# Scratch tiles placed by the plan, and the sums of the second norm's output made in the tiles of x

## The chip, the cores and the metric

The kernel runs on one core of a Trainium2 chip. The metric is the device time of one execution in microseconds (us), and lower is better. The kernel before takes 2038.9 us, the median of three runs (2038.4 to 2039.33). Engines go by their names in the profile: PE is TensorE, which multiplies matrices (PEld its weight loads), DVE is VectorE, ACT is ScalarE, POOL is GpSimd, and SP is SyncE, whose queue issues nearly all DMA transfers. Tiles lie in SBUF, with 128 partitions; matmuls write into PSUM, which has eight banks of 128 x 512 numbers.

## The reference, cut to what matters

The reference is a decoder trunk of two layers over 1024 tokens with 1024 channels, all in float32:

```python
for l in range(DEPTH):
    h = rmsnorm(x, attn_norm[l])
    proj = h @ w_in[l]                      # split into ten parts
    y_a = mla_attention(...)                # latent attention, 4 heads
    y_b = short_gated_conv(...)
    y_c = multiscale_pool(...)
    y_d = swa_sink_attention(...)           # sliding window
    mixed = ...                             # each group normed, times mix_norm
    x = x + mixed @ w_o[l]
    h2 = rmsnorm(x, ffn_norm[l])            # the second norm
    gate, up = jnp.split(h2 @ w_gate_up[l], 2, axis=-1)
    x = x + (jax.nn.silu(gate) * up) @ w_down[l]
return rmsnorm(x, final_norm)
```

where `rmsnorm(x, g)` is `x * rsqrt(mean(x * x) + eps) * g`. The change touches the second norm's output `h2`, in the form in which the gate and up products take it.

## The kernel before, in words

**Layout.** Activations are held transposed: channels on the 128 partitions, tokens along a row. A tile is 128 channels by 512 tokens, so x is eight channel blocks (d from 0 to 7) in two token halves (t is 0 or 1). Each float32 operand of a matmul is split into a high part, rounded to the matmul's input type by ACT, and the rest, which DVE gets by a subtraction (`split`, `half_split`, lines 362 to 380); `mm3` (line 344) then makes three matmuls of the parts.

**Stages of a layer.** First the combined projection and the four mixers, written interleaved; then the output projection with the residual (`out_part`, `out_last`), which leaves the new x in tiles `x[d][t]`, stores it to DRAM as `xr` (line 1271), squares it for the second norm, and splits it with the norm's gain into `hb`. Then the gate/up stage, in rounds over 22 blocks of the hidden channels, and then the down projection, which loads x again from `xr`.

**The gate/up products** go by a seven-product scheme for 2 x 2 blocks (channel parity by token half), in place of eight. Beside blocks of x it needs four combined blocks, called N1, N2, T3 and T4. `combine(j)`, line 1223, makes them for the channel blocks 2j and 2j + 1, so there are four rounds of it a layer. Of the round's four tiles of x, (a0, b0) is the even channel block in both token halves and (a1, b1) the odd one. With gains g0 and g1 it makes v0 = g0 b0 and v1 = g1 b1 on ACT (lines 1229 and 1230), and on DVE n1 = g0 a0 - v0 (line 1232), n2 = -n1 - v1 (line 1219, in `minus`), t3 = v1 - v0 (line 1238) and t4 = -g1 a1 - n2 (line 1240). Each of the four sums is then split (lines 364 and 367). At its end the four tiles of x are given back.

Between the rounds of `combine` the program has the first blocks' products: `plain` (line 1502) makes one block without the scheme, whose gates are multiplied by the norm (line 445), put through silu on ACT (line 1540), multiplied on POOL (line 1542) and multiplied with the up part on DVE (line 445 again); two further blocks, `early`, go through the scheme step by step (`start`, `n2`, `n1`, `t3`, `b22`, `t4`). `n2` needs N2 of all four rounds. The third such block, `GateUp(3)`, has its weights loaded at lines 1289 and 1291.

**Scratch.** Short-lived tiles of 128 x 512 numbers come from `tmp` (line 188), under one of three tags: `te`, with two buffers, `tn` and `tp`, with three each. A tile that asks for a buffer of its tag waits until the readers of that buffer's former tile are done. The longer-lived tiles come from 47 slots of two halves each (`Slots`, line 57; `u` in the profile); a slot is used again as the plan's times say.

**The order of the work** is the output of a planner that runs when the program is built (`Order`, `scheduled_kernel`, line 2210). The kernel is traced once with simple rules for places. A list scheduler with a cost for each instruction gives every instruction a planned end. From these ends come the PSUM bank of each `ps` tile (`banks`, line 2178) and the slots' uses; the kernel is traced again with them, scheduled again, and the order is improved with 30 tries of random changes (a fixed seed). This is done for two factors on the costs of DVE and ACT (`SLOW`, line 41); the version whose order takes least in six trials with random delays is kept, and its order is imposed on each engine's queue. The queues are worked off in that order on the chip: an instruction that waits holds up all behind it on its engine.

Of the kernel before, what the change touches and what calls it, by code (L numbers as in the profile page):

```python
# [14 lines left out]
F32 = mybir.dt.float32  # L15
F32R = mybir.dt.float32r
AF = mybir.ActivationFunctionType
ALU = mybir.AluOpType
AX = mybir.AxisListType

P = 128
# [3 lines left out]
HT = 512  # L25
# [9 lines left out]
B11, B21, B22, N1, N2, T3, T4, B12 = range(8)  # L35

HALVES = (1, 0)
OUT_PARTS = tuple((d, t) for d in range(NK) for t in HALVES)
N_U = 47
SLOW = (1.0, 1.03)  # L40
PREP = (1, 27)

# [83 lines left out]
def trunk_kernel(ctx: ExitStack, tc: tile.TileContext, ins, out, given=None, ends=None):  # L126
    nc = tc.nc
    act, dve, pe, pool, sp = nc.scalar, nc.vector, nc.tensor, nc.gpsimd, nc.sync
# [3 lines left out]
    tpool = ctx.enter_context(tc.tile_pool(name="tmp", bufs=6))  # L132
# [3 lines left out]

    slots = Slots(ctx.enter_context(tc.tile_pool(name="slots", bufs=1)), N_U, ends)
    R, F = View(slots, F32R), View(slots, F32)

    def rd(ap):  # L140
        return ap.bitcast(F32)
# [32 lines left out]
        "dc": deque(["t", "t", "mm", "mm"]),  # L174
    }

    bank_of = iter(given or ())

    def ps(tag):
        if tag in turns:  # L180
# [5 lines left out]
        return psum.tile([P, HT], F32, name=f"ps_{tag}", tag=b, bufs=1)  # L186

    def tmp(tag="te"):
        return tpool.tile([P, HT], F32, name=tag, tag=tag, bufs={"te": 2, "tn": 3, "tp": 3}[tag])

    def small(n):
        return spool.tile([P, n], F32, name=f"sm{n}", tag=f"sm{n}", bufs=16 if n < 16 else 2)
# [169 lines left out]
    def split(hi, lo, f, gain=None, after=None):  # L362
        if gain is None:
            a = act.copy(hi, f)  # L364
            if after is not None:
                behind(a, after)
            dve.tensor_tensor(out=lo, in0=f, in1=rd(hi), op=ALU.subtract)  # L367
        else:
            a = act.activation(hi, f, AF.Copy, scale=gain)  # L369
            dve.scalar_tensor_tensor(  # L370
                out=lo, in0=f, scalar=gain, in1=rd(hi), op0=ALU.mult, op1=ALU.subtract
            )
        return a

    def half_split(f, gain=None):
        h, l = R.half(), R.half()
        split(R.ap(h), R.ap(l), f, gain)
        return h, l
# [68 lines left out]
    def pcol(l, c, rows=slice(0, P)):  # L447
        return par[rows, l * PC_N + c : l * PC_N + c + 1]
# [65 lines left out]
    for l in range(L):  # L514
# [57 lines left out]
        if l == 0:  # L572
# [41 lines left out]
            for i in range(L):  # L614
                for o, c, n in ((nsink, PC_SINK, 4), (nffn, PC_FFN, NK)):
                    dve.tensor_scalar(
                        out=o[:, i * n : i * n + n],
                        in0=par[:, i * PC_N + c : i * PC_N + c + n],
                        scalar1=-1.0,
                        scalar2=None,  # L620
                        op0=ALU.mult,
# [17 lines left out]
        for t in range(2):  # L639
            f = tmp()  # L640
# [8 lines left out]
        for t in range(2):  # L649
            f = tmp()  # L650
# [5 lines left out]
            for g in range(2):  # L656
# [3 lines left out]
                    out=o[:, :, 1, :], in0=pv[:, :, g, :], in1=rd(o[:, :, 0, :]), op=ALU.subtract  # L660
# [187 lines left out]
        for ct in range(2):  # L848
            pp = nextp
            u, a, b = F.pair(), F.pair(), F.pair()  # L850
# [16 lines left out]
            else:  # L867
# [7 lines left out]
                out=dst,  # L875
                in0=src,
                scalar=cst[:, CC_INVW + ct : CC_INVW + ct + 1],
                in1=uf,
                op0=ALU.mult,
                op1=ALU.subtract,  # L880
# [28 lines left out]
        for m in range(2):  # L909
            pp = project() if m else nextp  # L910
            for t in range(2):
                f = tmp()
# [19 lines left out]
        for t in range(2):  # L932
            p = ps("s")
            for k in range(NK):
                for n in range(2):
# [4 lines left out]
                        start=k == 0 and n == 0,  # L940
# [6 lines left out]
            f = tmp()  # L947
# [267 lines left out]
        hb = [[None] * (NK // 2) for _ in range(8)]  # L1215
        ss2 = SumSq(D, True)

        def minus(o, a, b):
            dve.scalar_tensor_tensor(
                out=o, in0=a, scalar=-1.0, in1=b, op0=ALU.mult, op1=ALU.subtract  # L1220
            )

        def combine(j):

            (a0, b0), (a1, b1) = [[F.ap(x[2 * j + n][t]) for t in HALVES] for n in range(2)]
            c = PC_FFN + 2 * j
            g0, g1, n = pcol(l, c), pcol(l, c + 1), l * NK + 2 * j + 1
            v0, v1 = tmp("te"), tmp("te")
            act.activation(v0, b0, AF.Copy, scale=g0)
            act.activation(v1, b1, AF.Copy, scale=g1)  # L1230
            n1, n2, t3, t4 = tmp("tp"), tmp("tp"), tmp("tp"), tmp("tp")
            dve.scalar_tensor_tensor(
                out=n1, in0=a0, scalar=g0, in1=v0, op0=ALU.mult, op1=ALU.subtract
            )
            minus(n2, n1, v1)
            hb[N2][j] = half_split(n2)
            hb[N1][j] = half_split(n1)
            dve.tensor_tensor(out=t3, in0=v1, in1=v0, op=ALU.subtract)
            hb[T3][j] = half_split(t3)
            dve.scalar_tensor_tensor(  # L1240
                out=t4,
                in0=a1,
                scalar=nffn[:, n : n + 1],
                in1=n2,
                op0=ALU.mult,
                op1=ALU.subtract,
            )
            hb[T4][j] = half_split(t4)
            for n in range(2):
                for u in range(2):  # L1250
                    F.free(x[2 * j + n][u])
# [411 lines left out]
        r2.append(F.ap(ss2.rnorm(HALVES[0], tag="pv")))  # L1663
        plain_gates()
        combine(0)
        for w in early:
            w.split2()
        early[0].start()
        combine(1)
        r2.append(F.ap(ss2.rnorm(HALVES[1], tag="t")))  # L1670
        plain_acts()
        plain(1)
        early[1].start()
        combine(2)
        for hl in hb[B12]:
            for i in hl:
# [27 lines left out]
        for f in range(3, NFF):  # L1704
# [3 lines left out]
            end = f == NFF - 1  # L1708
# [75 lines left out]
        last = l == L - 1  # L1784
# [37 lines left out]
        banks = {}  # L1822
# [82 lines left out]
class Order:  # L1905
# [269 lines left out]
        found = (m for m in self.users if m.startswith(prefix) and m.rsplit("_", 1)[1].isdigit())  # L2175
        return sorted(found, key=lambda m: int(m.rsplit("_", 1)[1]))

    def banks(self, end):

        free, given = [0.0] * 8, []
        for m in self.tiles("ps_"):
            start = min(end[k] - self.cost[k][0] for k in self.users[m])
            b = max(range(8), key=lambda b: free[b] if free[b] <= start else -free[b])
            free[b] = max(end[k] for k in self.users[m])
            given.append(b)
        return given

# [20 lines left out]
def scheduled_kernel(fresh, ins_of, rounds=1):  # L2210

    def trace(banks, ends, order=None):
        nc = fresh()
        ins, out = ins_of(nc)
        with tile.TileContext(nc) as tc:
            asked = trunk_kernel(tc, ins, out, banks, ends)
            traced = [
                i  # L2220
                for i in nc.cur_bb.bb.instructions
                if Order.queue(i) in Order.ENGINES and i.opcode != "TilePoolBoundary"
            ]
            if order is not None:
                Order.impose(tc, traced, order)
        return nc, traced, asked

    nc, traced, asked = trace(None, None)
    first, tried, found = Order(traced, nc.dependency_edges), asked, []
    for slow in SLOW:  # L2230
        plan, asked, first.slow = first, tried, slow
        end = plan.find()[2]
        for _ in range(rounds):
            given = plan.banks(end), plan.ends(end, asked)
            nc, traced, asked = trace(*given)
            plan = Order(traced, nc.dependency_edges, slow)
            best = plan.find()
            end = best[2]
            order = plan.improve(best, 30)[1]
            found.append((plan.trial(order), given, order))  # L2240
    best = min(found, key=lambda x: x[0])
    return trace(*best[1], best[2])[0]
# [135 lines left out]
```

## Time and profile before

| | |
|---|---|
| median of three runs | 2038.9 us (2038.4 to 2039.33) |
| the profiled execution, first to last instruction | 2037.3 us; around it, to the median, 1.6 us |
| PE busy | 2022.8 us (99%) |
| DVE, ACT, POOL busy | 1541.0 (76%), 1020.8 (50%), 565.8 us (28%) |
| first layer's projections and mixers, up to the second norm's output | from 0 to about 386 us |
| its `combine` rounds | about 386 to 436 us |
| its gate/up rounds, then the down projection | to about 800, to about 1030 us |
| the second layer, the same stages | to about 1418, 1440, 1806 and 2037.3 us |

A row of the timeline has the start in us, the length in us (of several instructions, from the first to the last), the engine, the line, the operation, output and inputs by their names without numbers, shapes and a count; what stands in brackets is how long the engine was idle before it and what ended that. A row of the waits has who waited, for whom, the us in total, how many times and the longest. A row of the busy time by stretch has the stretch, its length, then busy us and number of instructions of PE, PEld, DVE, ACT and POOL, TensorE's granted clock, the share of the DMA engines that was busy, and GB/s. A row on a tile has the number of instructions, the shortest, median and longest in ns, and the first and last start.

### The profile page before, as it was taken

What the parts mean: (1) busy time and instruction counts of PE and PEld (TensorE: products, weight loads), DVE (VectorE), ACT (ScalarE), POOL (GpSimd) and SP (SyncE); (2) the same over time, 40 slices, a digit from 0 to 9 for tenths busy, and PEclk for the clock granted to TensorE, in tenths of its full rate; (3) what the DMA queues carried; (4) which work ended last, traced back from release to release, by engine and by line L of the source; (5) the groups of instructions that cost most, each with busy time, mean ns of one, the idle gap of its engine ahead of it and who ended that gap; (6) DMA issues with size and microseconds to landing.
All of it is one profiled execution on the core that took longest, in us unless ns stands there. A gap on an engine that the chain in (4) does not pass through costs nothing.

```text
span 2037.3 us, 26734 instructions
## 1 busy us (share of the span) xinstructions
PE 2022.8 (99%) x9418; PEld 1678.6 (82%) x9418; DVE 1541.0 (76%) x2442; ACT 1020.8 (50%) x1778; POOL 565.8 (28%) x428
## 2 busy tenths in 40 slices
PE   9999999999999999999999999999999999999998
PEld 7887888878888888888888878888888888888887
DVE  8779979997667768767646898889976766875555
ACT  7447657753333335555533676677433333354343
POOL 0100000047776782000001000000677777710000
PEclk9999999999999999999999999999999999999999
DMA  6431232434555546998835233242455555487552
GB/s 210 104 64 47 72 102 82 149 124 170 183 182 185 180 169 246 364 349 314 288 113 122 63 93 122 92 144 94 147 192 172 193 175 172 155 308 254 178 186 85
DMA packets 154087, 338.56 MB, mean 166 GB/s; under 512 B 14944, under 2 KB 62048, under 8 KB 153952
## 3 DMA queue, kind: packets, MB, share of 16 engines
q1 hardware_dynamic: 149472, 325.31, 46.3%
q0 software_dynamic: 4480, 11.54, 3.2%
q8 instruction: 74, 1.21, 0.3%
q14 instruction: 61, 0.50, 0.1%
HBM read 241.36 MB, written 105.91 MB: 170 GB/s over the span
## 4 chain that ended last, share of the span: by engine, by line
PE 95%; DVE 2%; DMA 1%; issue 1%; ACT 1%; POOL 0%; SPq 0%; DVEq 0%; POOLq 0%; ACTq 0%
PE ps_mm L344 37%; PE ps_s L344 28%; PE ps_t L344 12%; PE ps_pv L344 8%; PE ps_pv L1130 2%; PE ps_t L1118 1%; PE ps_s L1064 1%; PE ps_s L1066 1%; PE ps_s L1065 1%; PE ps_s L678 1%; PE ps_s L936 1%; PE ps_pv L739 1%; PE ps_t L727 1%; DVE u L367 1%; PE ps_t L424 0%
## 5 line engine op out<-in xcount | busy, mean ns | idle before, releaser
L344 PE MATMUL ps_mm<-u,u 128*128 128x512 f32 (+1 forms) x3378 | 832.4, 390 | 2.2 <-DVE tn L436 0.6
L344 PEld LDWEIGHTS ps_mm<-u,u 128*128 128x128 f32 x3378 | 617.4, 188 | 124.9 <-issue 3.1
L367 DVE TENSOR_TENSOR u<-u,u 128x1024 fp32r<-128x1024 f32 (+3 forms) x429 | 497.0, 1181 | 193.2 <-ACT u L364 131.4
L344 PE MATMUL ps_s<-u,u 128*128 128x512 f32 x2670 | 635.1, 390 | 0.7 <-ACT u L1358 0.5
L364 ACT CAST u<-u 128x1024 fp32r<-128x1024 f32 (+3 forms) x429 | 370.6, 882 | 438.6 <-PE ps_mm L344 62.4
L344 PEld LDWEIGHTS ps_s<-u,u 128*128 128x128 f32 x2670 | 501.5, 188 | 106.2 <-ACT u L1358 1.4
L344 PE MATMUL ps_t<-u,u 128*128 128x512 f32 (+1 forms) x1124 | 256.2, 378 | 0.1
L344 PEld LDWEIGHTS ps_t<-u,u 128*128 128x128 f32 x1124 | 202.7, 188 | 41.2 <-DVE u L1534 2.5
L1542 POOL TENSOR_TENSOR tp<-tp,u 128x512 f32<-128x512 f32 x80 | 126.9, 1586 | 347.8 <-ACT tp L1540 211.3
L344 PE MATMUL ps_pv<-u,u 128*128 128x512 f32 x744 | 177.3, 390 | 0.0
L344 PEld LDWEIGHTS ps_pv<-u,u 128*128 128x128 f32 x744 | 139.7, 188 | 28.9
L318 POOL DMA_DIRECT2D gd<-in_w_gu x24 | 21.2, 885 | 416.3 <-PE ps_t L344 280.9
L1127 POOL MEMSET u<- 128x128 f32 x32 | 6.3, 222 | 426.7 <-PE ps_pv L1130 117.6
L1540 ACT ACTIVATE tp<-tp 128x512 f32<-128x512 f32 x80 | 50.6, 632 | 131.5 <-DVE tp L445 131.4
L364 ACT CAST u<-ps_t 128x512 fp32r<-128x512 f32 (+3 forms) x132 | 64.6, 503 | 55.4 <-PE ps_t L1118 29.1
L367 DVE TENSOR_TENSOR u<-ps_t,u 128x512 fp32r<-128x512 f32 (+3 forms) x132 | 74.8, 581 | 13.9 <-ACT u L364 13.1
L1620 POOL TENSOR_TENSOR u<-u 128x352 f32<-128x352 f32 x64 | 79.3, 1240 | 9.8 <-DMA u<-in_w_dn 9.2
L369 ACT ACTIVATE u<-u,par 128x512 fp32r<-128x512 f32 x99 | 69.5, 717 | 23.3 <-DVE u L445 9.4
L1620 POOL TENSOR_TENSOR u<-u,u 128x352 f32<-128x352 f32 x64 | 76.7, 1199 | 2.6
L370 DVE SCALAR_TENSOR_TENSOR u<-u,par,u 128x512 fp32r<-128x512 f32 x99 | 72.9, 749 | 5.3 <-ACT u L369 5.2
L445 DVE TENSOR_TENSOR tp<-tp,u 128x512 f32<-128x512 f32 x76 | 73.9, 973 | 2.0
L1330 POOL TENSOR_TENSOR u<-u 128x512 f32<-128x512 f32 x38 | 67.4, 1773 | 27.3 <-DVE u L367 27.3
(209 smaller groups left out, 2316.6 us busy)
## 6 DMA issues: line engine op xcount, KB each, us to landing
u<-in_w_gu SPq DMA_DIRECT2D x84, 512.0 KB, 4.0
ad<-u SPq DMA_DIRECT2D x154, 256.0 KB, 2.3
u<-ad SPq DMA_DIRECT2D x70, 512.0 KB, 5.6
u<-in_w_dn SPq DMA_DIRECT2D x64, 352.0 KB, 3.5
qd<-u SPq DMA_DIRECT2D x64, 352.0 KB, 3.1
u<-in_w_in SPq DMA_DIRECT2D x43, 512.0 KB, 5.8
u<-qd SPq DMA_DIRECT2D x32, 512.0 KB, 5.4
u<-in_w_dn SPq DMA_DIRECT2D x24, 512.0 KB, 5.6
```

What stands on the lines that cost most here:

```text
L318: paced(pool.dma_start(d, a, **more))
L344: last_mm = pe.matmul(o, w, r, start=start and k == 0 and i == 0, stop=stop and k == n - 1 and i == 2, skip_group_check=again,)
L364: a = act.copy(hi, f)
L367: dve.tensor_tensor(out=lo, in0=f, in1=rd(hi), op=ALU.subtract)
L369: a = act.activation(hi, f, AF.Copy, scale=gain)
L370: dve.scalar_tensor_tensor(out=lo, in0=f, scalar=gain, in1=rd(hi), op0=ALU.mult, op1=ALU.subtract)
L445: dve.tensor_tensor(out=o, in0=a, in1=b, op=ALU.mult)
L1130: pe.matmul(py[:, c0:], v_of(j, h), R.ap(s)[:, c0:], start=j == 0 and n == 0, stop=j == nj - 1 and n == 1,)
L1330: pool.tensor_tensor(out=q4, in0=q4, in1=F.ap(self.raw[1] + 1), op=ALU.add)
L1540: last_silu = act.activation(g, g, AF.Silu)
L1542: pool.tensor_tensor(out=g, in0=g, in1=r, op=ALU.mult)
L1620: pool.tensor_tensor(out=o, in0=a, in1=b, op=ALU.add)
```

## The change

Scratch tiles are no longer taken from three tags. All go by one name (`tm`), and from the second trace on each is given one of eight places (`N_TMP`), which the function that gives out the PSUM banks now works out for scratch as well: among the places whose last user comes earlier in the program, the one that by the plan is freed last before the tile's first use, or, if none is free by then, the one that is free first. There were 2 + 3 + 3 = 8 buffers before, of the same size.

`combine` writes v0 and v1 over b0 and b1, n1 over a0, t3 over b0 and t4 over a1, and keeps one scratch tile, for n2; before it used six. Its arithmetic is the same.

```diff
+N_TMP = 8
...
-    bank_of = iter(given or ())
+    bank_of, tmp_of = map(iter, given or ((), ()))
...
     def tmp(tag="te"):
-        return tpool.tile([P, HT], F32, name=tag, tag=tag, bufs={"te": 2, "tn": 3, "tp": 3}[tag])
+        if given is None:
+            bufs = {"te": 2, "tn": 3, "tp": 3}[tag]
+            return tpool.tile([P, HT], F32, name="tm", tag=tag, bufs=bufs)
+        return tpool.tile([P, HT], F32, name="tm", tag=f"m{next(tmp_of)}", bufs=1)
...
-            v0, v1 = tmp("te"), tmp("te")
-            act.activation(v0, b0, AF.Copy, scale=g0)
-            act.activation(v1, b1, AF.Copy, scale=g1)
-            n1, n2, t3, t4 = tmp("tp"), tmp("tp"), tmp("tp"), tmp("tp")
+            act.activation(b0, b0, AF.Copy, scale=g0)
+            act.activation(b1, b1, AF.Copy, scale=g1)
+            n2 = tmp("tp")
             dve.scalar_tensor_tensor(
-                out=n1, in0=a0, scalar=g0, in1=v0, op0=ALU.mult, op1=ALU.subtract
+                out=a0, in0=a0, scalar=g0, in1=b0, op0=ALU.mult, op1=ALU.subtract
             )
-            minus(n2, n1, v1)
+            minus(n2, a0, b1)
             hb[N2][j] = half_split(n2)
-            hb[N1][j] = half_split(n1)
-            dve.tensor_tensor(out=t3, in0=v1, in1=v0, op=ALU.subtract)
-            hb[T3][j] = half_split(t3)
+            hb[N1][j] = half_split(a0)
+            dve.tensor_tensor(out=b0, in0=b1, in1=b0, op=ALU.subtract)
+            hb[T3][j] = half_split(b0)
             dve.scalar_tensor_tensor(
-                out=t4,
+                out=a1,
                 in0=a1,
                 scalar=nffn[:, n : n + 1],
                 in1=n2,
                 op0=ALU.mult,
                 op1=ALU.subtract,
             )
-            hb[T4][j] = half_split(t4)
+            hb[T4][j] = half_split(a1)
...
-    def banks(self, end):
+    def places(self, end, prefix, n):
-        free, given = [0.0] * 8, []
-        for m in self.tiles("ps_"):
+        free, last, given = [0.0] * n, [-1] * n, []
+        for m in self.tiles(prefix):
             start = min(end[k] - self.cost[k][0] for k in self.users[m])
-            b = max(range(8), key=lambda b: free[b] if free[b] <= start else -free[b])
+            b = max((b for b in range(n) if last[b] < self.users[m][0]), key=lambda b: free[b] if free[b] <= start else -free[b])
             free[b] = max(end[k] for k in self.users[m])
+            last[b] = self.users[m][-1]
             given.append(b)
         return given
...
-            given = plan.banks(end), plan.ends(end, asked)
+            given = (plan.places(end, "ps_", 8), plan.places(end, "tm_", N_TMP)), plan.ends(end, asked)
```

## The prediction

> **What bounds the kernel now.** I read the page's head, then the busy time by stretch, then who TensorE waited for, then the other engines' waits, then the timeline where TensorE stood.
>
> ```profile
> span 2037.3 us, 26734 instructions
> PE 2022.8 (99%) x9418; PEld 1678.6 (82%) x9418; DVE 1541.0 (76%) x2442; ACT 1020.8 (50%) x1778; POOL 565.8 (28%) x428
> ```
>
> TensorE (PE) is idle for 2037.3 - 2022.8 = 14.5 us in all. By stretch (length, then the busy us of PE, weight load, DVE, ACT, POOL):
>
> ```profile
> 0.00:386.00 386.00, 383.74 (x1877) 317.31 (x1878) 334.96 (x747) 246.74 (x530) 13.90 (x32) 1.00 0.35 106
> 386.00:436.00 50.00, 49.14 (x212) 39.25 (x211) 45.55 (x69) 33.15 (x54) 9.95 (x6) 1.00 0.21 72
> 436.00:800.00 364.00, 363.95 (x1605) 300.79 (x1604) 266.76 (x259) 130.86 (x178) 255.32 (x178) 1.00 0.53 179
> 1030.00:1418.00 388.00, 386.63 (x1910) 322.38 (x1909) 311.26 (x713) 233.21 (x508) 15.13 (x29) 1.00 0.35 105
> 1418.00:1440.00 22.00, 21.71 (x96) 17.66 (x95) 20.39 (x31) 15.41 (x26) 6.00 (x3) 1.00 0.34 108
> 1440.00:1806.00 366.00, 365.95 (x1612) 302.12 (x1611) 266.93 (x260) 131.76 (x179) 262.39 (x180) 1.00 0.52 178
> 2010.00:2037.30 27.30, 17.72 (x141) 16.87 (x139) 9.81 (x20) 7.07 (x16) 0.00 (x0) 0.88 0.27 92
> ```
>
> The idle time of these rows is 2.26, 0.86, 0.05, 1.37, 0.29, 0.05 and 9.58 us, together 14.46: the stretches left out have none. The granted clock is 1.00 until the tail, so the clock takes nothing. The last row is the tail, in which the last norm has no matmul beside it.
>
> ```profile
> PE ps_pv L575 <- DVE ones L149: 1.1, 1, 1.1
> PE ps_mm L344 <- DVE tn L436: 0.6, 1, 0.6
> PE ps_mm L344 <- ACT u L369: 0.6, 1, 0.6
> PE ps_s L431 <- ACT tn L430: 0.5, 1, 0.5
> PE ps_s L344 <- ACT u L1358: 0.5, 2, 0.3
> PE ps_t L424 <- ACT u L364: 0.5, 1, 0.5
> PE ps_mm L344 <- ACT u L364: 0.4, 1, 0.4
> PE ps_mm L344 <- DVE u L370: 0.3, 1, 0.3
> PE ps_s L344 <- DVE u L367: 0.2, 1, 0.2
> PE ps_s L1064 <- DVE te L445: 0.2, 1, 0.2
> ```
>
> These are all of TensorE's waits. The first is the start and L431 is the tail; what is left in the middle is 0.6 + 0.6 + 0.5 + 0.5 + 0.4 + 0.3 + 0.2 + 0.2 = 3.3 us in nine waits; by stretch it was 14.46 - 9.58 - 1.1 = 3.8, and I take the larger. Idle time tells a little too little, because a matmul counts as busy longer than the next one has to wait. In the steady stage twelve take 2.72 us, 0.227 each:
>
> ```profile
> 510.86 2.72 PE ps_mm L344 x12
> ```
>
> So of the six that start at 421.13 (rows below) the last one's slot ends at 422.49, and the next starts at 423.10: 0.61 lost where the row says 0.44 idle. With 0.17 more for each of nine waits, what TensorE loses in the middle is 3.8 + 1.5 = 5.3 us. The rest is matmuls at their rate, and the change takes no matmul away. **The floor for this change is 2038.9 - 5.3 = 2033.6 us.** The sum is made against the profiled execution, 2037.3; the median of the runs, 2038.9, lies 1.6 above it, and I add that at the end.
>
> **Part 1: scratch places from the plan.** Before, a `te` tile waits for one of two buffers, `tn` and `tp` for one of three each; after, any tile takes any of eight, as the plan's times say. No instruction goes. What can go is a wait of a writer for the last reader of the buffer's former tile. Such waits, in the whole run, are the first three of these rows (L755, L408 and L435 write `tn`; L756, L1146 and L439 read it):
>
> ```profile
> ACT tn L755 <- DVE u L756: 3.8, 7, 0.9
> ACT tn L408 <- DVE u L1146: 2.1, 2, 1.3
> ACT tn L435 <- DVE u L439: 1.3, 1, 1.3
> ...
> DVE u L1534 <- POOL tp L1542: 30.3, 17, 2.7
> DVE u L445 <- POOL tp L1542: 2.4, 2, 1.2
> ```
>
> That is at most 7.2 us on ACT, which is idle for half of the run, and no such row on DVE, the fullest helper engine (335 of the first 386 us). ACT's slack covers them: in the same stretch it is idle for 386 - 247 = 139 us. None of TensorE's ten rows names a release of scratch; where they name `tn` or `te` it is a result, or a bank that is read out. I cost the direct gain at 0, between ends of 0 (it is all covered) and 5.3 (all that TensorE waits for).
>
> **Part 2: the sums in the tiles of x.** `combine` asks for one scratch tile in place of six. The same two ACT products, four DVE sums and their splits stay, with the same shapes, so no duration changes. The new waits are those of writing over x: the store to `xr`, the square and the split must have read it.
>
> ```profile
> 387.37 0.92 SPq L1271 DMA_DIRECT2D xr<-u  x2
> 418.09 0.72 ACT L1229 ACTIVATE te<-u,par 128x512 f32<-128x512 f32 x1
> ```
>
> The last stores of layer 0 are issued at 387.4 and the last round's first product, the one that will write over x, runs at 418.1: 31 us behind. The earlier rounds write over tiles that were stored earlier, in the same order. Cost 0; the cover is DVE's own backlog, which makes the rounds run so long behind the stores.
>
> What is left is the order around `combine`, where scratch was scarce. Layer 0, last round:
>
> ```profile
> 421.13 1.53 PE L344 MATMUL ps_mm<-u,u 128*128 128x512 f32 x6
> 421.65 0.75 DVE L1232 SCALAR_TENSOR_TENSOR tp<-u,par,te 128x512 f32<-128x512 f32 x1
> 422.48 3.41 POOL L1542 TENSOR_TENSOR tp<-tp,u 128x512 f32<-128x512 f32 x1 [13.45 <-ACT tp L1540]
> 423.10 2.82 PE L344 MATMUL ps_mm<-u,u 128*128 128x512 f32 x10 [0.44 <-ACT u L364]
> ...
> 425.92 0.69 DVE L445 TENSOR_TENSOR u<-ps_s,tp 128x512 f32<-128x512 f32 x1 [1.19 <-POOL tp L1542]
> 426.53 0.68 DVE L367 TENSOR_TENSOR u<-tp,u 128x512 fp32r<-128x512 f32 x1
> ...
> 427.26 1.20 PE L344 MATMUL ps_s<-u,u 128*128 128x512 f32 x4 [0.21 <-DVE u L367]
> ...
> 428.67 5.75 PE L344 MATMUL ps_s<-u,u 128*128 128x512 f32 x24 [0.21 <-ACT u L1358]
> ```
>
> L1232 makes n1, L1219 n2. TensorE stands at 423.10 for the split of n1, and at 427.26 for that of n2, which sits in DVE's queue behind L445, which stands 1.19 us for POOL's gate product. Here the gate and the combine's tiles share the three `tp` buffers, which limits the orders that the planner may write. With free places n1 and n2 can come earlier, or L445 later. But DVE has 45.55 us of work in these 50 us and nothing of it goes; n1 was not standing for a buffer, DVE was busy. Ends: 0, and the 0.86 + 0.29 us of idle time of both layers plus 0.17 for each of their waits (five), 2.0 us. I take 0.5, near the lower end, since the row of DVE's load speaks for it. Below nothing it can go as well, by the rivals.
>
> **Part 3: a new plan.** Names and dependences change, so all queues are ordered anew, with the same random draws on another graph. Nothing in the trace prices that. Nearest rows: the 3.3 us of TensorE's waits are what one plan of this planner leaves. Another leaves between 0 and about twice as much; I take the same, cost 0, ends -5.3 and +5.3.
>
> Sum: 2037.3 - 0 - 0.5 + 0 = 2036.8 us profiled, and with 1.6 around it **2038.4 us**.
>
> **The rivals.**
>
> *Reuse drawn tight (slower).* Of the places free at a tile's planned start, the new rule takes the one freed last. So tiles follow each other closely, and a reader that is late on the chip holds up the next writer, on an in-order queue. Such readers are late: POOL's product L1542 took 3.41 above, where the row of all of them has
>
> ```profile
> L1542 POOL TENSOR_TENSOR tp<-tp,u x80: 1279/1299/3409, 406.5 to 1818.4; 128x512 f32<-128x512 f32 x80
> ```
>
> In the gate/up stage that does no harm: DVE stood 30.3 us in 17 waits for POOL there, and TensorE lost 0.05 us a layer. Where DVE is full it does: the one wait of 1.19 us on L445 went with 0.38 + 0.38 = 0.76 us on TensorE (427.26 and 428.67, each 0.21 and 0.17). It decides from six new waits of that kind on DVE in the 846 us of the four fuller stretches (6 x 0.76 = 4.6 us); with eight it is 2038.4 + 6.1 = 2044.5 us. Against it: banks of PSUM are given by the same rule already, and TensorE's rows show under 4 us of it. Chance 0.16.
>
> *The gate products starve (slower).* If free places make DVE's sums denser, POOL's products beside them go like that of 3.41 us, not like 1.30. Some four of the six POOL instructions of the stretch from 386 are such products, so eight in both layers; by the row of L445 one a layer holds DVE up now; if the other six do too, it is 6 x 0.76 = 4.6 us, 2043.0. For it: the product ended 1.2 us after DVE fell idle at 424.7, as if it ran only then. Against it: L445 itself ends DVE's rush as soon as it waits. Chance 0.04. The Trainium skill, "SBUF — State Buffer", section "SBUF: two separate sides", says that a DVE operation with two SBUF inputs and a GpSimd operation exclude each other for a whole instruction; by that alone one DVE sum would hold the product up once, some 0.7 us by the rows here, not 2.1, so the trace shows a longer wait than one instruction's, and this rival would be worth a third.
>
> *x held longer, weights late (slower).* The halves of x are now free only behind the splits, some 3 us later, and loads take such places.
>
> ```profile
> 428.68 0.38 SPq L1289 DMA_DIRECT2D u<-in_w_gu  x1
> ```
>
> ```profile
> 445.30 2.72 PE ps_pv L344 x12
> ```
>
> ```profile
> u<-in_w_gu SPq DMA_DIRECT2D x84, 512.0 KB, 4.0
> ```
>
> The load for the first round after the two early ones goes out at 428.7 and its first matmuls run at 445.3, 16.6 us later. It lands 4.0 us after issue; a split of it takes another few us (an ACT cast and a DVE subtraction, between 0.6 and 2 us each in these stretches, in busy queues), so 8 in all by estimate: 3 us more are covered, from 9 on they are not, and at 13 it is 4.1 us, 2042.5. Chance 0.02.
>
> *All waits go (faster by over 0.2%).* 4.1 of the 5.3 us would have to go, in the attention stretches too, where no row names scratch: 2034.3 us. Chance 0.08.
>
> **How the numbers follow.** My forecast, within 0.2% (4.1 us, about what a measurement can tell from no change), has 0.70, with its own range 2035 to 2043; the slower rivals 0.22, the faster one 0.08. The likeliest time is 2038.4. The range goes down to 2034.5, close to the floor, and up to the tight reuse with nine waits, 2038.4 + 6.8 = 2045.2; about 0.07 lies below or at the floor and 0.1 above.
>
> **What would show it.** Right: PE busy within 2 us of 2022.8 and the gate/up rows again within 0.1 us of full; the waits of ACT for DVE on `tn` gone or renamed; no new DVE row behind scratch over 3 us. n1, t3 and t4 rows writing and reading `u` alone. Part 2 is right if the idle 0.86 and 0.29 us of the combine stretches shrink. Wrong: a PE row over 2 us in the attention stretches behind a DVE or ACT write of scratch (tight reuse), L445 waits for POOL four times or more at over 1 us (starving), or a weight load as TensorE's releaser behind `combine` (x held).

## The result, and the profile after

The kernel after takes 2043.28 us (median; 2042.45 to 2044.23) against 2038.69 for the kernel before on the same chip: 1.0023 times as long, with an interval of 1.0015 to 1.003. It is slower, by 4.6 us. The prediction said 2038.4 and most likely no change.

The head of the page of the kernel after:

```profile
span 2041.1 us, 26855 instructions
PE 2026.1 (99%) x9418; PEld 1675.0 (82%) x9418; DVE 1555.2 (76%) x2442; ACT 1023.1 (50%) x1778; POOL 577.5 (28%) x428
```

TensorE is idle for 2041.1 - 2026.1 = 15.0 us, which is 0.5 more than before. But it is *busy* for 3.3 us longer, with the same 9418 matmuls. A matmul of 128 x 512 is recorded as 0.39 us long by the mean of its rows, and the next one starts 0.227 us after it in the steady stage, so a pause shorter than the difference is booked as busy time. By the starts in the two traces the median distance of these matmuls is 0.227 us in both: the rate has not changed, the pauses have. Most of the 3.8 us between the two profiles is there. The Trainium skill, "Perfetto Trace Analysis", section "Identifying the Most-Contended Engine", says that matmul busy % is not a good measure of how close a kernel is to its roofline, because pipelined instructions look smaller in the trace. The trace agrees on the percentage, which is 99% before and after, but not on the reason: here the recorded lengths run over the next start. With a fixed number of matmuls the busy *microseconds* do tell: up by 3.3.

The busy time by stretch of the kernel after, the same stretches as in the prediction:

```profile
0.00:386.00 386.00, 382.41 (x1858) 312.30 (x1859) 329.70 (x740) 242.72 (x524) 13.90 (x32) 1.00 0.36 105
386.00:436.00 50.00, 50.00 (x221) 41.22 (x220) 48.59 (x74) 35.20 (x59) 10.98 (x5) 1.00 0.25 85
436.00:800.00 364.00, 364.00 (x1606) 301.07 (x1605) 273.66 (x260) 132.51 (x179) 262.44 (x179) 1.00 0.53 178
1030.00:1418.00 388.00, 387.56 (x1908) 320.55 (x1907) 312.54 (x715) 236.13 (x513) 15.16 (x29) 1.00 0.36 104
1418.00:1440.00 22.00, 21.99 (x98) 17.77 (x97) 20.81 (x29) 12.32 (x20) 7.63 (x3) 1.00 0.37 120
1440.00:1806.00 366.00, 364.62 (x1604) 300.36 (x1603) 273.42 (x262) 129.66 (x176) 261.79 (x179) 1.00 0.53 175
2010.00:2041.10 31.10, 21.52 (x169) 20.42 (x167) 12.20 (x25) 8.00 (x18) 0.00 (x0) 0.93 0.31 110
```

Read the counts behind PE's busy time: they say how much work a stretch got done. In the first 386 us, the first layer's projections and mixers, 1858 matmuls start where it was 1877. Those 19 are about 4 us late (386 / 1877 = 0.206 us each), of which the idle time shows 1.33 (382.41 against 383.74). In the `combine` stretch it is 221 where it was 212: 9 are won back, about 2 us, and the idle time there is gone, 0.86 to 0.00. In the second layer's `combine` it goes from 0.29 to 0.01. The gate/up stretch of the first layer is full as before; that of the second starts 8 matmuls fewer, about 1.8 us (8 x 0.227), and is idle for 1.38 us where it was 0.05. So about 4 us are lost, 2 won back and 2 lost again, close to the 3.8 us between the profiles. At 2010.00 us 169 matmuls are still to do; it was 141. The tail's idle time is 9.58 us in both.

So the sums did locally what they were meant to, and something far from them cost more: the mixers of the first layer lie ahead of the first `combine` and hold no line of it (of the places they do use scratch).

TensorE's waits after (who waited, for whom, us in total, times, longest) hardly show it:

```profile
PE ps_pv L579 <- DVE ones L150: 1.1, 1, 1.1
PE ps_s L348 <- ACT tm L1411: 1.0, 1, 1.0
PE ps_s L682 <- DVE u L663: 0.9, 1, 0.9
PE ps_s L435 <- ACT tm L434: 0.5, 1, 0.5
PE ps_s L1068 <- DVE tm L440: 0.5, 1, 0.5
PE ps_t L348 <- DVE u L1537: 0.4, 2, 0.2
PE ps_mm L348 <- DVE u L1271: 0.3, 1, 0.3
PE ps_t L658 <- DVE u L663: 0.2, 1, 0.2
PE ps_mm L348 <- ACT u L373: 0.2, 1, 0.2
PE ps_pv L1134 <- ACT u L368: 0.2, 1, 0.2
```

Without the start and L435 (the tail) that is 3.7 us in nine waits. Before, it was 3.3. The longest two are chains that came a little late. The timeline of the first mixers gives one (lines are 3 or 4 higher than before):

```profile
45.18 0.68 DVE L562 SCALAR_TENSOR_TENSOR tm<-ps_s,u 128x512 f32<-128x512 f32 x1
...
45.79 3.67 PE L348 MATMUL ps_mm<-u,u 128*128 128x512 f32 x15
...
49.04 0.69 DVE L569 TENSOR_TENSOR u<-tm,u 64x512 fp32r<-64x512 f32 x1
49.76 0.43 DVE L663 TENSOR_TENSOR u<-ps_t,u 128x256 fp32r<-128x256 f32 x1
50.21 0.69 DVE L572 TENSOR_TENSOR u<-tm,u 64x512 fp32r<-64x512 f32 x1
50.30 0.52 PEld L682 LDWEIGHTS ps_s<-u,u 128*128 128x128 f32 x4 [1.25 <-issue]
50.33 0.63 PE L682 MATMUL ps_s<-u,u 128*128 128x128 f32 x4 [0.86 <-DVE u L663]
```

The scores of L682 need the split L663. It starts on DVE as soon as L569, ahead of it in the queue, is done (no bracket: DVE was not idle) and ends at 50.19. The 15 matmuls that the plan put ahead of the scores ended at 49.46, 0.7 us too soon. No scratch tile is waited for here.

The other, 1.0 us of the 1.38 in the second layer's gate/up stretch:

```profile
1461.92 0.68 DVE L449 TENSOR_TENSOR tm<-tm,u 128x512 f32<-128x512 f32 x1
...
1462.63 0.63 ACT L1543 ACTIVATE tm<-tm 128x512 f32<-128x512 f32 x1 [5.87 <-DVE tm L449]
...
1463.17 0.57 ACT L1411 COPY tm<-ps_s 128x512 f32<-128x512 f32 x1
...
1463.79 0.50 PE L348 MATMUL ps_s<-u,u 128*128 128x512 f32 x1 [1.00 <-ACT tm L1411]
```

TensorE stands until L1411 has copied out a PSUM bank. L1411 is behind the silu L1543 in ACT's queue, and that had stood for DVE's product L449, its input. That too is a matter of the order, not of a place.

### The profile page after: what moved, and what is told of

Read it like the earlier page. It is cut to its first block, busy times and chain, and to the rows that moved or that the text cites. A ratio compares the mean times of both kernels' runs of the same rounds, so it can differ in the third digit from the quotient of the medians.

```text
span 2041.1 us, 26855 instructions
## 1 busy us (share of the span) xinstructions
PE 2026.1 (99%) x9418; PEld 1675.0 (82%) x9418; DVE 1555.2 (76%) x2442; ACT 1023.1 (50%) x1778; POOL 577.5 (28%) x428
## 4 chain that ended last, share of the span: by engine, by line
PE 86%; DVE 6%; issue 2%; ACT 2%; DMA 2%; POOL 1%; SPq 0%; DVEq 0%; POOLq 0%; ACTq 0%
PE ps_mm L348 33%; PE ps_s L348 27%; PE ps_t L348 10%; PE ps_pv L348 7%; PE ps_pv L1134 2%; PE ps_t L1122 1%; DVE u L371 1%; PE ps_s L1068 1%; PE ps_s L1069 1%; PE ps_s L1070 1%; DVE u L374 1%; PE ps_s L682 1%; PE ps_pv L743 1%; PE ps_t L731 1%; DVE u L420 0%
## 5 line engine op out<-in xcount | busy, mean ns | idle before, releaser
L371 DVE TENSOR_TENSOR u<-u,u 128x1024 fp32r<-128x1024 f32 (+3 forms) x453 | 505.5, 1139 | 189.0 <-ACT u L368 119.0
L368 ACT CAST u<-u 128x1024 fp32r<-128x1024 f32 (+3 forms) x453 | 385.9, 869 | 406.8 <-DVE u L371 62.9
L1545 POOL TENSOR_TENSOR tm<-tm,u 128x512 f32<-128x512 f32 x80 | 142.1, 1776 | 317.3 <-ACT tm L1543 317.3
L1543 ACT ACTIVATE tm<-tm 128x512 f32<-128x512 f32 x80 | 50.6, 632 | 152.2 <-DVE tm L449 152.1
L1623 POOL TENSOR_TENSOR u<-u,u 128x352 f32<-128x352 f32 x64 | 82.8, 1294 | 1.1
L412 ACT ACTIVATE tm<-u 128x512 f32<-128x512 f32 (+1 forms) x91 | 53.8, 599 | 49.2 <-DVE u L1814 41.4
L449 DVE TENSOR_TENSOR tm<-tm,u 128x512 f32<-128x512 f32 x76 | 74.5, 980 | 2.2
```

The costliest lines, as they stand in the source:

```text
L412: act.activation(q, f, AF.Square)
L449: dve.tensor_tensor(out=o, in0=a, in1=b, op=ALU.mult)
L1543: last_silu = act.activation(g, g, AF.Silu)
L1545: pool.tensor_tensor(out=g, in0=g, in1=r, op=ALU.mult)
L1623: pool.tensor_tensor(out=o, in0=a, in1=b, op=ALU.add)
```

## The experiments

A word on what is varied. The planner makes a plan for each factor in `SLOW` (1.0 and 1.03 times the costs of DVE and ACT) and keeps the one that does better in its own six trials. The rival theories: (a) the change itself costs, by tight reuse of places (the prediction's rival; theory A in the expectations) or by its `combine` (theory C); (b) the change is harmless or good, and the planner drew a worse plan (theory B) or picked the worse of its two (theory D, from the second group of runs on).

### One part alone, and other random draws

`combine_alone` is the kernel before with only `combine` changed: v0 and v1 over b0 and b1, n1 over a0, t3 over b0, t4 over a1.

```diff
...
-            n1, n2, t3, t4 = tmp("tp"), tmp("tp"), tmp("tp"), tmp("tp")
+            n2 = tmp("tp")
...
```

> Part 2 without part 1: the four sums in the tiles of x, scratch under its three tags as before. Theory A, reuse drawn tight: the loss is part 1's, so this run is at 2038.7 us or 1 to 2 us faster (2036.5 to 2038.9). Theory B, a new plan: each change of the graph gives another order, so the time lies anywhere from 2034 to 2044, with no relation to the part. Theory C, writing over x costs: this run is as slow as the changed kernel, 2043.

`places_alone` is the kernel before with only the places changed; `combine` keeps six scratch tiles.

```diff
...
-        return tpool.tile([P, HT], F32, name=tag, tag=tag, bufs={"te": 2, "tn": 3, "tp": 3}[tag])
...
+        return tpool.tile([P, HT], F32, name="tm", tag=f"m{next(tmp_of)}", bufs=1)
...
```

> Part 1 without part 2: scratch places from the plan, the sums in six scratch tiles as before. Theory A, reuse drawn tight: 2043 us or slower (2043 to 2048), since more tiles now share the eight places. Theory B, a new plan: anywhere from 2034 to 2044. Theory C, writing over x costs: 2038.7.

`before_seed2` and `after_seed2` change the random draws of the planner's tries.

```diff
-        draw = random.Random(1)
+        draw = random.Random(2)
```

> The kernel before, with another seed for the random tries that improve its order; no other change. Theory A, reuse drawn tight: the order as such is worth little, so within 1.5 us of 2038.7. Theory B, a new plan: it moves by some us, as the change did, and slower rather than faster (2036 to 2044).

> The changed kernel, with another seed for the random tries that improve its order; no other change. Theory A, reuse drawn tight: still 2042 to 2045, since the places are given before the tries. Theory B, a new plan: anywhere from 2036 to 2046, with some chance of below 2040.

| kernel | us (lowest to highest) | ratio to before, with its interval |
|---|---|---|
| `combine_alone` | 2036.85 (2035.44 to 2037.65) | 0.9991, 0.9981 to 1.0 |
| `places_alone` | 2042.2 (2040.88 to 2043.37) | 1.0018, 1.0009 to 1.0027 |
| `before_seed2` | 2038.78 (2038.2 to 2039.42) | 1.0, 0.9991 to 1.001 |
| `after_seed2` | 2034.69 (2033.32 to 2036.44) | 0.9981, 0.9971 to 0.9991 |

The loss seemed to come with the places. No theory had all four right: tight reuse (A) had `combine_alone` and `before_seed2`, a new plan (B) had `combine_alone` and `places_alone` (`before_seed2` lay in its range, but did not move as it said), and `after_seed2` came out below every range. The same changed kernel, with another draw, is 8.6 us faster than with the first and 4 us faster than the kernel before. Its stretches (first mixers, first `combine`):

```profile
0.00:386.00 386.00, 383.39 (x1877) 317.15 (x1878) 334.02 (x747) 247.81 (x530) 13.71 (x32) 1.00 0.36 106
386.00:436.00 50.00, 50.00 (x222) 41.17 (x221) 47.21 (x70) 33.39 (x54) 13.10 (x5) 1.00 0.24 79
```

The first stretch is back at 1877 matmuls, and `combine` keeps its gain. What costs 19 matmuls there is thus no property of the change.

### The factor

Which of its two plans had the planner kept? These runs force one factor.

```diff
-SLOW = (1.0, 1.03)
+SLOW = (1.03,)
```

> The changed kernel with SLOW = (1.03,), seed 1: the plan made with DVE and ACT counted 3% slower is the only candidate. Theory D, the pick: the planner makes two plans, and the change itself is good; the changed kernel lost because its pick went to the plan made with the factor 1.0, while the kernel before and after_seed2 run the one made with 1.03. Then this run is at 2034 to 2037 us. Theory B, a new plan is a lottery with any seed and factor: anywhere from 2034 to 2044. Theory A, reuse drawn tight: 2042 to 2045, since the places are given by the same rule.

> Scratch places from the plan, the sums in six scratch tiles, SLOW = (1.03,). places_alone, which had 2042.2, runs the plan made with 1.0. Theory D, the pick: 2035 to 2038.5. Theory B, lottery: anywhere from 2034 to 2044. Theory A, reuse drawn tight: 2042 or slower.

```diff
-SLOW = (1.0, 1.03)
+SLOW = (1.0,)
```

> The kernel before with SLOW = (1.0,): the plan that it did not pick. Theory D, the pick: 5 to 9 us slower than the kernel before, 2043 to 2048. Theory B, lottery: anywhere from 2036 to 2044, no side given. Theory A, reuse drawn tight: 2038.7 within 1.5 us, since its scratch rotates under tags with either factor.

> The sums in the tiles of x, scratch under its tags, SLOW = (1.0,). combine_alone, which had 2036.85, runs the plan made with 1.03. Theory D, the pick: slower than combine_alone by 4 to 9 us, 2041 to 2046. Theory B, lottery: anywhere from 2034 to 2044. Theory A, reuse drawn tight: 2036.9 within 1.5 us.

And, with the other draws as well (`random.Random(2)` and 1.0):

> The changed kernel with SLOW = (1.0,) and seed 2. Theory D, the pick (plans made with plain costs run slow on the chip): 2041 to 2046, like the changed kernel itself, which is the plan of factor 1.0 with seed 1 (2043.3). Rival, a lottery of plans at any factor: anywhere from 2034 to 2046, with an even chance of below 2040.

> The kernel before with SLOW = (1.0,) and seed 2. Theory D, the pick: 2044 to 2050, like before_100 (2046.7). Rival, a lottery of plans at any factor: anywhere from 2036 to 2050, with an even chance of below 2043.

The order of the instructions on all five queues gives the rest of the table: the kernel before is the program that it becomes with 1.03 alone, and the kernel after is the one that it becomes with 1.0 alone. **The pick flipped.** The ranges given for theory D held, but for two: `combine_100` is 3 us above its range, and `places_103` 1.1 us above its own. Medians in us; the ratios of the runs made for this were 0.9992 (0.9983 to 1.0002) for `after_103`, 1.0004 (0.9994 to 1.0013) for `places_103`, 1.0039 (1.0024 to 1.0054) for `before_100`, 1.0053 (1.0038 to 1.0068) for `combine_100`, 1.0029 (1.0019 to 1.004) for `after_100_seed2` and 1.005 (1.0033 to 1.0067) for `before_100_seed2`:

| | plan at 1.0 | plan at 1.03 | kept by the planner |
|---|---|---|---|
| before | 2046.66 | 2038.7 | 1.03 |
| `combine` alone | 2049.08 | 2036.85 | 1.03 |
| places alone | 2042.2 | 2039.57 | 1.0 |
| both (after) | 2043.28 | 2036.96 | 1.0 |
| before, second draw | 2049.2 | 2038.78 | 1.03 |
| after, second draw | 2044.49 | 2034.69 | 1.03 |

Read by rows: in all six the plan at 1.03 is faster, by 2.6 to 12.2 us. Read by columns: at one factor and one draw, the changed kernel is faster than the kernel before, by 3.4 and 4.7 us at 1.0 and by 1.7 and 4.1 at 1.03. So the change is worth some 3.5 us by these four pairs (their mean; for the 1.7 alone the interval still holds no change). In the pair measured first it is 1.7 us won by the change and 6.3 lost by the pick, together the 4.6. The two parts can't be priced one by one in this way: `combine` gives +2.4 at 1.0 and -1.8 at 1.03, the places -4.5 and +0.9; that the signs differ may be the scatter of single plans.

The place of the loss agrees in part. The matmuls started in the first 386 us are 1855 (before, second draw), 1858 (after), 1859 (its second draw), 1865 (`places_alone`), 1866 (before) and 1870 (`combine` alone) with plans at 1.0, and 1873 to 1878 with plans at 1.03. But `combine` alone loses most elsewhere: 3 matmuls here, against 36 in the second layer's mixers (1875 at 1.0, 1911 at 1.03). `after_100_seed2`, `combine_100`, then `after_103` and its `combine`:

```profile
0.00:386.00 386.00, 382.29 (x1859) 313.33 (x1860) 330.57 (x740) 242.49 (x524) 13.95 (x32) 1.00 0.36 105
```

```profile
0.00:386.00 386.00, 383.84 (x1870) 315.08 (x1871) 331.41 (x742) 243.82 (x526) 14.26 (x32) 1.00 0.36 105
```

```profile
0.00:386.00 386.00, 383.87 (x1877) 317.06 (x1878) 334.10 (x746) 247.71 (x530) 14.05 (x32) 1.00 0.36 106
386.00:436.00 50.00, 50.00 (x222) 41.34 (x221) 47.74 (x70) 33.57 (x55) 14.76 (x7) 1.00 0.24 79
```

`combine_100` has 383.84 us of busy time in that stretch, practically what the kernel before had, and 7 matmuls fewer: the pauses booked as busy time again.

Why did it pick the slower one? These are the planner's own ratings (its model's times, not measurements) of its two plans, as it rates them, and rated again with DVE and ACT 3% slower:

```
            at the plain costs      with DVE and ACT 3% slower
            1.0       1.03          1.0       1.03
before      2022.8    2021.1        2037.8    2026.7
combine     2023.6    2019.7        2039.0    2024.3
places      2020.4    2022.7        2033.9    2027.8
after       2019.0    2020.5        2034.4    2025.2
```

At the plain costs the two lie within 4 us of each other, and the wrong one leads by 1.5 for the kernel after and by 2.3 for the places alone. With 3% more, the eight ratings stand in the order of the eight measured times above, of which the first two are only 0.1 us apart. The second draw's plans have the ratings 2023.2 and 2022.0 (before) and 2020.0 and 2020.0 (after) at the plain costs, and 2038.7 and 2026.6, 2035.3 and 2024.4 with 3% more. With 3% more all twelve stand as on the chip but for three pairs of neighbours. The plain rating gives the changed kernel's two plans of that draw the same, so `after_seed2` got the good one by luck. So the rating at the plain costs is what misleads: the chip behaves as if there were less time to spare on the helper engines than the costs say. What it is that the costs leave out, the runs don't show.

### More room, and a better judge

`after_106` gives more room than any plan so far.

```diff
-SLOW = (1.0, 1.03)
+SLOW = (1.06,)
```

> The changed kernel with SLOW = (1.06,), seed 1: DVE and ACT planned 6% slower in place of 3%. Theory D, the pick, with room as the reason (the chip's DVE and ACT are a little slower than the planner's costs, so a plan with the plain costs runs late everywhere): not slower than after_103, 2034 to 2037.5. Rival, the factor 1.03 is merely another draw of the plan: nothing ties 1.06 to 1.03, 2034 to 2046.

`after_judged` and `before_judged` make 16 plans (four factors, four draws) and rate them all with 2% on DVE and ACT.

```diff
-SLOW = (1.0, 1.03)
+SLOW = (1.0, 1.03, 1.04, 1.06)
+SEEDS = (1, 2, 3, 4)
+JUDGE = 1.02
...
-        if fixed is None:
+        f = self.slow if fixed is None else JUDGE
+        if f != 1.0:
...
-            order = plan.improve(best, 30)[1]
-            found.append((plan.trial(order), given, order))
+            for seed in SEEDS:
+                order = plan.improve(best, 30, seed)[1]
+                found.append((plan.trial(order), given, order))
```

> The changed kernel with its judge mended: four factors (1.0, 1.03, 1.04, 1.06) with four seeds each, and the trials that pick among the sixteen count DVE and ACT 2% slower. Theory D, with room as the reason: the pick goes to a plan with room, 2033 to 2036, faster than the kernel before. Rival, the trials can't tell plans apart: 2034 to 2046, about the mean of what was seen, 2039.

> The kernel before with the same mended judge and the same sixteen candidates, nothing of the change in it. If the change is worth something with plans of the same quality: 1 to 4 us slower than after_judged, 2035.5 to 2038.5. If only the pick mattered: equal to after_judged within 1 us.

| kernel | us (lowest to highest) | ratio to before, with its interval |
|---|---|---|
| `after_106` | 2033.67 (2033.13 to 2034.21) | 0.9975, 0.9965 to 0.9985 |
| `after_judged` | 2033.74 (2032.97 to 2034.65) | 0.9976, 0.9966 to 0.9986 |
| `before_judged` | 2038.57 (2036.48 to 2040.77) | 0.9998, 0.9988 to 1.0007 |

Both versions of the changed kernel beat both kernels of this case, by 5 us and 9.6; `after_106` is even 0.3 us below its range. The same judge gives the kernel before nothing, so the change is worth 4.8 us there, a little more than the 1 to 4 expected and than the pairs above. The head of `after_106`, and its first mixers, first `combine` and second mixers:

```profile
span 2032.4 us, 26891 instructions
PE 2019.8 (99%) x9418; PEld 1677.3 (83%) x9418; DVE 1534.6 (76%) x2442; ACT 1021.3 (50%) x1778; POOL 572.7 (28%) x428
```

```profile
0.00:386.00 386.00, 383.04 (x1879) 317.21 (x1880) 336.13 (x748) 246.96 (x530) 13.75 (x32) 1.00 0.37 106
386.00:436.00 50.00, 50.00 (x222) 41.16 (x221) 46.64 (x70) 33.86 (x55) 7.55 (x6) 1.00 0.24 79
1030.00:1418.00 388.00, 387.50 (x1919) 324.06 (x1918) 315.26 (x717) 237.50 (x515) 14.67 (x29) 1.00 0.37 105
```

TensorE is idle for 12.6 us in all, and busy for 6.3 us less than in the kernel after, with the same matmuls. In the second mixers it is as idle as there (0.50 and 0.44 us) and starts 11 matmuls more.

### Is tight reuse harmful at all?

`longest_103` takes, of the scratch places that are free, the one free for longest in place of the one freed last, with the factor 1.03. PSUM's banks keep their rule.

```diff
-            b = max(..., key=lambda b: free[b] if free[b] <= start else -free[b])
+            b = max(..., key=lambda b: (free[b] if prefix == "ps_" else 1e6 - free[b]) if free[b] <= start else -free[b])
```

> The changed kernel with SLOW = (1.03,) and another rule for scratch alone: of the places free at a tile's planned start, the one that has been free longest, in place of the one freed last. Theory A, reuse drawn tight: faster than after_103 (2037.0) by 2 us or more, 2033 to 2035. Theory D: tight reuse costs nothing much, so 2035 to 2038.5.

It takes 2041.44 us (2039.21 to 2044.07), 1.0014 of before (1.0004 to 1.0023): 4.5 us *slower* than `after_103` and above both ranges. Loose reuse should have been the faster one if tight reuse held queues up. Its loss lies in the second mixers, idle for 3.11 us:

```profile
1030.00:1418.00 388.00, 384.89 (x1890) 318.85 (x1889) 310.55 (x708) 235.54 (x511) 15.76 (x29) 1.00 0.35 104
```

It is a single plan, and the other plans at 1.03 lie up to 4.9 us apart (2034.69 to 2039.57). So it doesn't show that loose reuse is bad; it only gives tight reuse no support as a cost.

### Room on which engine?

`after_dve` and `after_act` put the factor 1.03 on one engine's costs only.

```diff
-SLOW = (1.0, 1.03)
+SLOW = (1.03,)
...
-                (a * self.slow, b * self.slow) if e in ("DVE", "Activation") else (a, b)
+                (a * self.slow, b * self.slow) if e == "DVE" else (a, b)
```

> The changed kernel with the factor 1.03 on DVE's costs alone, ACT at 1.0. If what the plans lack is room for DVE, the fuller of the two engines: near after_103, 2034 to 2038.5. If it is room for ACT: near the changed kernel, 2041 to 2045.

The other has `e == "Activation"` in that place.

> The changed kernel with the factor 1.03 on ACT's costs alone, DVE at 1.0. If what the plans lack is room for DVE: near the changed kernel, 2041 to 2045. If it is room for ACT: 2034 to 2038.5. If either will do, since most chains run through both: both this run and after_dve at 2035 to 2039.

DVE alone: 2042.47 us (2041.35 to 2044.1), 1.002 of before (1.001 to 1.0029). ACT alone: 2038.96 (2037.09 to 2040.76), 1.0002 (0.9993 to 1.0011). With room on neither it is 2043.28, with room on both 2036.96. The room on ACT, an engine half idle, was worth 4.3 us, that on DVE, the fullest helper, 0.8. `after_act` lies 0.5 us above the range given for room on ACT. It is one plan each, so the split may be scatter in part. Why ACT's room should help stays open.

## Why the prediction was wrong

**What bounds the kernel** held: TensorE, at 99%, clock at 1.00 until the tail, and nothing but small waits to win. The floor, 2033.6, did not: that the best versions reached 2033.67 and 2033.74, and no less, is luck. `after_106` is still idle for 2.4 us between start and tail (12.6 - 9.1 - 1.1), so a plan without waits would lie lower. The reading "idle time tells a little too little", for which I added 0.17 us for each *listed* wait, went for too little, and "the rest is matmuls at their rate" was wrong: pauses too short to be listed are the larger part. From after to `after_106`, 2.4 us of idle time went and 6.3 us of busy time.

**Part 1, cost 0.** Nothing shows a direct gain or loss: no row of DVE's waits names a reader of scratch that holds up a writer. ACT's wait for the reader of a scratch tile is what it was (L759 was L755; 3.8 us in 7 waits before):

```profile
ACT tm L759 <- DVE u L760: 3.6, 7, 0.7
```

**Part 2, gain 0.5, ends 0 and 2.0.** Right in mechanism, too small in size. The sign named for it came: the idle times 0.86 and 0.29 became 0.00 and 0.01, and 9 more matmuls start in the first of the two stretches. `combine_alone` was 1.8 us faster, close to the upper end, though that is also another plan. I leaned on DVE's load, 45.55 of 50 us, as the reason why nothing could go; after, DVE does 48.59 us in that stretch, so it wasn't at its limit. The gain is not the edit's alone, though. With six scratch tiles that stretch had between 47.80 and 49.15 us of busy time in six kernels (the lowest is `places_103`, first row below), but in `before_judged` (second row) another order filled it too; with one it was 50.00 in nine kernels, and 49.61 and 49.56 in the two others, both at 1.0.

```profile
386.00:436.00 50.00, 47.80 (x206) 37.89 (x205) 44.94 (x66) 31.90 (x53) 6.66 (x5) 1.00 0.23 75
```

```profile
386.00:436.00 50.00, 50.00 (x218) 40.52 (x218) 47.52 (x70) 33.73 (x55) 6.69 (x5) 1.00 0.22 74
```

Writing over x cost nothing that the traces show: no load appears among the releasers of TensorE's waits.

**Part 3, the new plan, cost 0, ends -5.3 and +5.3: the step that failed.** I priced it as noise around nothing, from TensorE's 3.3 us of waits, "what one plan of this planner leaves". What the runs show in its place is a choice of one from two plans, of which the one at 1.0 was the slower in six pairs of six. The kernel before had the better of its two, by 8 us, so a new pick had more to lose than to win. The kernel after got its worse one, by 6.3 us, and the term that I put at 0 measured that. The net 4.6 happens to lie inside the ends, but the size came from the wrong row, and the equal ends on both sides from no row. The text of the kernel names both factors; what neither the page nor the trace could tell is that the plan at 1.0 is the slow one in each case.

**Rivals.** *Tight reuse* (2044.5) is near the measured time and isn't its cause: the same rule runs in `after_103`, `after_seed2`, `after_106` and `after_judged`, all of them at or below the kernel before, and the looser rule was slower. Nor did its sign appear: no row of TensorE's waits is over 1.0 us in the middle. Its price of 0.76 us was too high as well: the wait at 428.67 was for L1358, which had itself stood for matmuls of TensorE, so the trace ties only the first 0.38 to L445. *The gate products starve*: L445, now L449, should have waited for POOL four times or more at over 1 us. It did once:

```profile
DVE u L449 <- POOL tm L1545: 1.2, 1, 1.2
```

*x held longer*: not seen (by its own rows the uncovered time at 13 us would be 13 - 8.6 = 4.4 us, not 4.1). *All waits go* (2034.3): not in this plan, but `after_seed2`, `after_106` and `after_judged` came to 2033.7 to 2034.7; I said that the attention stretches would have to gain too, and in `after_106` they did, though by only 2 matmuls in the first and 9 in the second (1910 before).

**Signs.** "PE busy within 2 us of 2022.8" failed, at 2026.1, and was the best of the signs: it is where most of the time went. "Gate/up rows within 0.1 us of full" held for the first layer and failed for the second (364.62 of 366).

## What to carry to other kernels

Where a planner writes the order, an edit's time is the edit plus a new draw from the planner: force the same factor and the same seed on both kernels, in two or three pairs, before a word is said on the edit (here -1.7 to -4.7 us in four pairs, under a measured +4.6). Try plans made and rated with costs a few per cent above the measured ones: here the rating with 3% more put eight plans in the order in which they ran on the chip, while the one at plain costs took a plan that was 6.3 us slower. And where TensorE is full, compare its busy microseconds and its matmuls started by a given time too, not only its idle time and its list of waits.

## What the runs showed of the hardware that I had not expected

**A POOL product can stretch to 4.8 times its shortest length while TensorE stays busy.** The row of all products L1545 of the kernel after (shortest, median and longest in ns), then POOL's timeline and DVE's at the longest, in the first `combine`:

```profile
L1545 POOL TENSOR_TENSOR tm<-tm,u x80: 1286/1588/6123, 407.7 to 1821.1; 128x512 f32<-128x512 f32 x80
```

```profile
420.00 6.12 POOL L1545 TENSOR_TENSOR tm<-tm,u 128x512 f32<-128x512 f32 x1 [10.80 <-ACT tm L1543]
```

```profile
419.53 0.68 DVE L371 TENSOR_TENSOR u<-tm,u 128x512 fp32r<-128x512 f32 x1
420.13 3.62 DVE L371 TENSOR_TENSOR u<-u,u 128x512 fp32r<-128x512 f32 x5
423.68 0.68 DVE L1241 TENSOR_TENSOR u<-u,u 128x512 f32<-128x512 f32 x1
424.28 0.68 DVE L371 TENSOR_TENSOR u<-u,u 128x512 fp32r<-128x512 f32 x1
425.87 1.33 DVE L371 TENSOR_TENSOR u<-u,u 128x1024 fp32r<-128x1024 f32 x1 [0.91 <-ACT u L368]
```

One DVE operation is running when POOL's product starts, seven more follow without a gap, until 424.96, and POOL ends 1.16 us after that, about the 1.29 us of the shortest product. It looks as if POOL got nothing until DVE stood still. The Trainium skill, "SBUF — State Buffer", section "SBUF: two separate sides", says that such a pair locks each other out for a whole instruction. The trace agrees that they exclude each other, and shows more: here a run of instructions back to back kept POOL out as one. In `longest_103` the longest product took 9.85 us. TensorE lost little or nothing by it: that stretch of the kernel after is 50.00 of 50.00 us busy, with 221 matmuls started where 222 is the most in any run.

**Most of the gap between two plans can sit in pauses that no view lists.** From `after_106` to the kernel after, the same 9418 matmuls are busy for 6.3 us longer, while the idle time, which is what the waits list, grows by 2.4. It isn't so in each pair: of the 4.7 us that the profile of `longest_103` is longer than that of `after_103`, 3.0 are idle time (15.7 against 12.7).
